# An encoder block on one core: later value products, a filled last stretch, a one-pass turn and a two-piece last store

## The chip, the cores and the metric

The kernel runs on one core of a Trainium2 chip. The metric is the device time of one launch in microseconds (us), the median of several runs. A core has TensorE (matrix products, with a weight load ahead of each), VectorE, ScalarE, GpSimd, SyncE (which here only issues transfers) and 16 DMA engines. The profile calls them PE, PEld, DVE, ACT, POOL and SP; SPq and ACTq are the transfers issued from SyncE and from ScalarE.

## The reference

One layer over 1024 rows of 1024 numbers, in float32:

```
h = x @ W_in                                   # q, k, v, z of two groups of 8 heads
y_a = neighborhood_attention(q_a, k_a, v_a)    # 16 x 64 grid, window 8 x 16, learned bias
y_b = windowed_gqa(rotary(q_b), rotary(k_b), v_b, sink)   # |i - j| <= 128
mixed = concat(y_a * silu(z_a), y_b * silu(z_b))
x = layer_norm(alpha * x + mixed @ W_out) * gain + bias
```

## The kernel before, in words

Every float32 factor is split into two float16 parts, high and low, and a product is made of three float16 products (high·high, high·low, low·high). The splits need scales, which come from maxima over the whole tensors.

**Opening.** The values of the first 512 rows are made while x is read in. Meanwhile VectorE reduces x to one maximum for each partition (`xm`, then `gm`). `x_turn` brings the 128 maxima of `gm` into every partition with one float32 product against the identity, `x_scale` takes the maximum of the result and works out the scale `xsc`, and `x1_hi` scales x with it for the float16 products that follow. The order of this part is the order in which it is written.

**Middle.** 128 attention units run in numbered steps: scores on TensorE, softmax on VectorE and ScalarE, then the probabilities, split in two, are turned by DMA transposes (L999, tile `tr`). Four units are a quad. The value product of quad q (`stage_pv`, L1035, 24 products) takes the turned probabilities and is put at the step that `PV_AT` gives; `stage_z` (L1046, VectorE) multiplies its result into the gate `z` at the step in `Z_AT`. Quads 30 and 31 are the last two. Between these steps `pump_to` feeds TensorE other products: first the projections (L404), then the head of the output projection (`out_head`, L1165), which can already use the four groups of gated results that are ready (`m4` to `m7`). `FILL_AT` and `FILL_N` say how many such products are fed by which step; what is left in the list comes after the last step, and `LO` is how many steps follow the last unit.

**End.** `final` splits the other four groups (`m0` to `m3`: cast on ScalarE L1076, difference on VectorE L1077, in halves of 512 rows) and the rest of the output weights (`wo8` to `wo15`: L1121/L1123, L1129/L1131), and finishes the output projection, 24 products for each of `m0` to `m3` over the eight sums that are open, then the row blocks 3 to 7 that have none yet. VectorE adds the residual, takes the statistics and normalises. Within `final` a scheduler with a model of the engines sets the order of the instructions, so it can differ from the order of the code.

**The last row block** (`norm_last`) has only its own time ahead of the end. Its first `NPE` columns go over TensorE: the normalised row is a product with a diagonal matrix `dg` (L1247) onto the bias, copied out by ScalarE (L1251) and stored from ScalarE's queue (L1252). The other columns go over VectorE in two operations (L1248, L1249) and are stored from SyncE's queue (L1250).

Of the kernel before, what the change touches and what calls it, by code (L numbers as in the profile page):

```python
# [13 lines left out]
ALU = mybir.AluOpType  # L14

S = 1024
D = 1024
# [21 lines left out]
SCALE_AT = ((4, 6), (7, 2))  # L39
K_ORDER = (5, 0, 6, 1, 7, 2, 3, 4)  # L40
FILL = ORDER[NPRO:]
FILL_AT = [0, 6.6, 13.4, 21.4, 29.4, 37.4, 45.4, 53.4, 61.4, 70, 78.8, 87.6, 96.4, 105, 113, 122, 125, 127, 128.5, 131.5, 136]
ZTAG = {"z3": "zv", "zb3": "zc", "z2": "zs", "zb1": "zd", "zb2": "ze"}
X2POOL = (1, 3, 5)
WVPOOL = (3, 5)
# [7 lines left out]
WO_MAX = 88  # L53
EO = (4, 5, 6, 7, 0, 1, 2, 3)
LAST = ((0, 384), (384, 128))
NPE = 384
PRE_AT = (12, 20)
WARP = (0, 0.33, 0.54, 0.86, 1)
QK_AT = 0.75
# [15 lines left out]
def hybrid_block(ctx, tc, xT, x, wt, wv, wo, bias, sink, gain, lbias, cos, sin, bmask, out):  # L75
    nc = tc.nc
# [10 lines left out]
    def bank(tag):  # L87
        bufs = {"pj": 2, "s": 5, "t": 1}[tag]
        return (ps1 if bufs == 1 else ps2).tile([128, 512], F32, tag=tag, name=f"ps_{tag}", bufs=bufs)
# [21 lines left out]
    def zslot(name, tag="z"):  # L111
        return zp.tile([128, S], F32, tag=tag, name=name, bufs=3 if tag == "z" else 1)
# [268 lines left out]
    def project(name):  # L381
        n = ORDER.index(name)
        w_split(2 * n + 2)
        for half in range(2):
            ps = new_group()
            for k in range(KT):
                if k % 4 == 0:
                    need(w_ops[2 * n + k // 4])
                h, l = parts[2 * n + k // 4]
                if n + 2 < NPRO and half == 0 and k == 4:  # L390
                    w_scan(2 * n + 4)
                if n + 2 < NPRO and half == 1 and k == 0:
                    w_scan(2 * n + 5)
                if half == 0 and k == 4:
                    w_split(2 * n + 3)
                if n + 2 < NPRO and half == 1 and k == 3:
                    z_tree(n + 2)
                if n + 2 < NPRO and half == 1 and k == 7:
                    w_scale(n + 2)
                for i, (a, b) in enumerate(((h, x16h), (h, x16l), (l, x16h))):  # L400
                    mv = b[half, k]
                    if name[0] == "q" and name[1] != "b":
                        mv = mv.rearrange("p (r b c) -> p b r c", b=4, r=8)
                    nc.tensor.matmul(ps, a[:, k % 4, :], mv,  # L404
                                     start=(k == 0 and i == 0), stop=(k == KT - 1 and i == 2))
                    if not (k == KT - 1 and i == 2):
                        yield
            groups.append(evac(name, half, ps))
            yield
# [26 lines left out]
    with ExitStack() as vctx:  # L436
# [76 lines left out]

        def x_turn(ps):
            nc.tensor.matmul(ps[:, 320:448], gm.to_broadcast([128, 128]), identf, start=False, stop=True,
                             skip_group_check=True)

        def x_scale(ps):
            nc.vector.tensor_reduce(gm, ps[:, 320:448], axis=AXX, op=ALU.max)
# [97 lines left out]
        for k in range(KT):  # L617
            if k + 3 < KT:
                ahead(k + 3)
            if k + 4 == KT:  # L620
                for j in range(KT):
                    nc.sync.dma_start(x1[j], xT[1, j])
                x_max(6, xh[6].bitcast(F32))
            for ps in FIRST if k == 0 else SECOND if k == 1 else ([(t, a, i) for i in range(3)] for t, a in T1):
                for t, a, i in ps:
                    lh, rh = ((xh, wvh), (xl, wvh), (xh, wvl))[i]
                    nc.tensor.matmul(banks[t, a][:, :320], lh[k][:, 128 * t:128 * t + 128],
                                     rh[k][:, 320 * a:320 * a + 320],
                                     start=(k == 0 and i == 0), stop=(k == KT - 1 and i == 2))
                if k > 1:  # L630
                    g = T1.index((t, a))
                    if (k, g) == SCALE_AT[0]:
                        wv_scale(banks[t, a])
                        for j in range(KT):
                            wv_hi(j)
                        x_max(7, xh[7].bitcast(F32))
                        for j in range(4):
                            x_max(8 + j, x1pair[j])
                        nc.vector.tensor_reduce(gm, xm, axis=AXX, op=ALU.max)
                        wv_lo(0)  # L640
                    if (k, g) == SCALE_AT[1]:
                        x_turn(banks[t, a])
                        x_scale(banks[t, a])
                        nc.vector.tensor_scalar(vo, vo, xrs, 0.5, op0=ALU.mult, op1=ALU.mult)
# [405 lines left out]
        at(WIN_AT[b], window, b)  # L1050
    run_to(48 * NPRO)
    fill.extend(project(n) for n in FILL)
    FILL_N = [48] * len(FILL) + [9, 9, 6, 12, 24]
    pumped = [0]

    def pump_to(u):
        n = 0
        k = int(u) % 4
        u = int(u) // 4 * 4 + 4 * (WARP[k] + (WARP[k + 1] - WARP[k]) * (u - int(u)))
        for k, c in enumerate(FILL_N):  # L1060
            u0, u1 = FILL_AT[k], FILL_AT[k + 1]
            n += int(c * min(max((u - u0) / (u1 - u0), 0), 1))
# [87 lines left out]
            m_ops[e].append(enq("pool", lambda h=h: nc.gpsimd.tensor_sub(  # L1150
                ml[e][:, h], zt[e][:, h], mh[e][:, h]), o))

    LO = 10
    NU = len(units)
    def out_mms(t, a, ps, es, c=None):
        o, w = (0, 512) if c is None else LAST[c]
# [25 lines left out]
    def final():  # L1182
# [15 lines left out]
        gb, bb = gain_tile[0], zslot("bb")  # L1198
# [19 lines left out]
        def row_stats(t):  # L1218
            mv = fp.tile([128, 2], F32, tag="mv", name="mv")
            nc.vector.bn_aggr(mv, stats[t][:, :4 if t == 7 else 2, :])  # L1220
            sd = fp.tile([128, 1], F32, tag="sd", name="sd")
            nc.scalar.activation(sd, mv[:, 1:2], AF.Sqrt, bias=eps, scale=ALPHA ** 2)  # L1222
            return mv, sd
# [9 lines left out]
        def norm_last(t):  # L1233
            ts = slice(128 * t, 128 * t + 128)
            xr = xrs[t]
            h0, h1 = slice(0, NPE), slice(NPE, D)
            ga = fp.tile([128, D], F32, name="ga", bufs=1)
            nc.scalar.mul(ga, gb, ALPHA)
            mv, sd = row_stats(t)
            ps = bank("t")  # L1240
            nc.tensor.matmul(ps[:, :NPE], identf, bb[:, h0], start=True, stop=False)
            nc.vector.scalar_tensor_tensor(xr[:, h0], xr[:, h0], mv[:, 0:1], ga[:, h0], op0=ALU.subtract, op1=ALU.mult)  # L1242
            rstd = fp.tile([128, 1], F32, tag="rstd", name="rstd")
            nc.vector.reciprocal(rstd, sd)
            dg = fp.tile([128, 128], F32, name="dg", bufs=1)
            nc.scalar.mul(dg, identf, rstd)
            nc.tensor.matmul(ps[:, :NPE], dg, xr[:, h0], start=False, stop=True)  # L1247
            nc.vector.scalar_tensor_tensor(xr[:, h1], xr[:, h1], mv[:, 0:1], ga[:, h1], op0=ALU.subtract, op1=ALU.mult)  # L1248
            nc.vector.scalar_tensor_tensor(xr[:, h1], xr[:, h1], rstd, bb[:, h1], op0=ALU.mult, op1=ALU.add)  # L1249
            nc.sync.dma_start(out[ts, h1], xr[:, h1])  # L1250
            nc.scalar.copy(xr[:, h0], ps[:, :NPE])  # L1251
            nc.scalar.dma_start(out[ts, h0], xr[:, h0])  # L1252

# [46 lines left out]
        with tc.manual_schedule():  # L1300
            norm_last(7)
# [17 lines left out]
        stage_mm(us)  # L1319

    PV_AT = {4 * q + 11: q for q in range(30)}
    PV_AT.update({131: 30, 135: 31})
    Z_AT = {4 * q + 13: q for q in range(30) if q not in (24, 25, 28, 29)}
    Z_AT.update({115: 24, 116: 25, 128: 28, 129: 29, 132: 30, 136: 31})

    clock["step"] = 0
    scan_ops = []
    for i in range(-LD, NU + LO):
        if 0 <= i + LD < NU:
# [162 lines left out]
```

## Time and profile before

| | us |
|---|---|
| median of 3 runs | 439.92 (439.67 to 441.48) |
| profiled execution, its own time | 441.73 |
| span of the profiled execution | 439.9 |
| TensorE busy in the span | 431.2 (98%) |
| VectorE | 347.8 (79%) |
| ScalarE | 298.8 (68%) |
| GpSimd | 212.7 (48%) |

The profile is of one execution, whose own time is 1.83 us longer than its span and 1.81 us longer than the median. Rows of the timeline give start, duration, engine, line, the operation with its result and operands, and how many were merged; a bracket gives the idle time ahead and what ended it. "x3" after a shape is a count of three.

### The profile page before, as it was taken

Reading aid. Unit: us, or ns where it says so; the run is one execution under the profiler, and the core shown is the slowest. Engines: PE = TensorE matmul, PEld = TensorE weight load, DVE = VectorE, ACT = ScalarE, POOL = GpSimd, SP = SyncE. Lnnn points to the kernel's source line nnn. Section 1 sums busy time; section 2 is a strip of 40 time slices with the busy share of each in tenths; the row PEclk is TensorE's granted clock in tenths of the full one; section 3 lists DMA queues with packets and bytes.
Section 4 is the critical chain, followed back from the end, with each engine's and each line's share of the span. In section 5 each row is a group of like instructions: output and inputs, shape, how many; then the busy total and the mean of one; then the engine's idle time right before and its main releaser. Section 6 shows DMA issues by size and latency. Waiting matters only on the chain. (4 is left out here: it accounts for less than half of the span.)

```text
span 439.9 us, 8798 instructions
## 1 busy us (share of the span) xinstructions
PE 431.2 (98%) x2955; PEld 233.2 (53%) x2955; DVE 347.8 (79%) x897; ACT 298.8 (68%) x697; POOL 212.7 (48%) x204
## 2 busy tenths in 40 slices
PE   9999999999999999999999999999999989999994
PEld 8987754444444545454545455554545544444442
DVE  5999947929989988988888887887879739089954
ACT  6798359877577988877889899879787756002211
POOL 0305743564845868356333455566652158005840
PEclk9999999999999999999999999999999999999999
DMA  8992088967946978776999899999999979101721
GB/s 296 343 339 71 5 259 250 302 247 254 322 113 136 168 147 171 141 145 143 173 154 201 138 190 223 192 202 217 216 208 225 193 166 363 41 1 72 262 74 72
DMA packets 133981, 81.72 MB, mean 186 GB/s; under 512 B 101296, under 2 KB 113328, under 8 KB 133680
## 3 DMA queue, kind: packets, MB, share of 16 engines
q1 hardware_dynamic: 133504, 80.67, 74.4%
q8 instruction: 23, 0.38, 0.3%
q10 hardware_dynamic: 432, 0.49, 0.3%
q14 instruction: 22, 0.18, 0.1%
HBM read 50.73 MB, written 9.96 MB: 138 GB/s over the span
## 5 line engine op out<-in xcount | busy, mean ns | idle before, releaser
L404 PE MATMUL ps_pj<-xf,wh 128*128 128x512 f16 x672 | 201.2, 379 | 0.0
L404 PE MATMUL ps_pj<-xf,wl 128*128 128x512 f16 x336 | 127.5, 380 | 0.0
L404 PEld LDWEIGHTS <-wh 128*128 128x128 f16 x672 | 64.9, 98 | 75.4 <-issue 0.8
L1165 PEld LDWEIGHTS <-m 128*128 128x128 f16 x408 | 38.7, 98 | 43.7
L974 ACT ACTIVATE ps_s<-sn,nm 128x385 f32<-128x385 f32 (+3 forms) x96 | 52.1, 543 | 13.9 <-DVE nm L958 12.5
L992 ACT ACTIVATE split<-ps_s,ri 128x384 f16<-128x384 f32 (+2 forms) x96 | 48.5, 539 | 18.3 <-ACT ps_s L974 11.7
L993 DVE SCALAR_TENSOR_TENSOR split<-ps_s,ri,split 128x384 f16<-128x384 f32 (+2 forms) x96 | 52.0, 570 | 5.6 <-ACT split L992 4.6
L1165 PE MATMUL ps_s<-wo,m 128*128 128x512 f16 (+1 forms) x240 | 53.3, 374 | 0.0
L404 PEld LDWEIGHTS <-wl 128*128 128x128 f16 x336 | 32.8, 98 | 38.5 <-issue 0.3
L219 POOL TENSOR_SCALAR wr<-wr,wsc 128x512 f32<-128x512 f32 x26 | 22.4, 862 | 46.9 <-ACT wh L214 45.5
L958 DVE CUSTOM_DVE_ANT_0 sn<-ps_s,bm,nsk 128x384 f32<-128x384 f32 (+1 forms) x64 | 39.7, 635 | 6.6 <-PE ps_s L933 6.4
L901 POOL TENSOR_SCALAR bias<-bias,rsg 128x552 f32<-128x552 f32 (+1 forms) x24 | 20.0, 834 | 45.8 <-DMA bias<-in_bias 33.9
L958 DVE CUSTOM_DVE_ANT_0 sn<-ps_s,bias,sg 128x264 f32<-128x264 f32 (+1 forms) x64 | 33.9, 543 | 2.3 <-PE ps_s L933 1.6
L933 PE MATMUL ps_s<-ks,qs 64*128 64x384 f16 (+4 forms) x384 | 33.4, 305 | 0.1
L220 POOL TENSOR_TENSOR wl<-wr,wh 128x512 f16<-128x512 f32 x26 | 31.8, 1223 | 2.2
L1222 ACT ACTIVATE sd<-mv,eps 128x1 f32<-128x1 f32 x8 | 2.4, 295 | 41.8 <-DVE mv L1220 39.5
L1264 POOL TENSOR_TENSOR xr<-xr,gb 128x512 f32<-128x512 f32 x7 | 11.2, 1607 | 35.9 <-ACT xr L1261 35.9
L993 DVE SCALAR_TENSOR_TENSOR split<-px,ri,split 128x384 f16<-128x384 f32 (+2 forms) x32 | 26.0, 812 | 2.5 <-ACT split L992 2.4
L933 PEld LDWEIGHTS <-qs 64*128 64x128 f16 x384 | 16.2, 94 | 19.5 <-issue 13.3
L681 PEld LDWEIGHTS <-xf 128*128 128x128 f16 x216 | 21.0, 98 | 8.5 <-DVE xf L535 0.3
L1165 PE MATMUL ps_pj<-wo,m 128*128 128x512 f16 (+1 forms) x120 | 24.2, 347 | 0.0
L681 PE MATMUL ps_s<-wf,xf 128*128 128x320 f16 x144 | 23.8, 299 | 0.0
(213 smaller groups left out, 791.0 us busy)
## 6 DMA issues: line engine op xcount, KB each, us to landing
ws<-in_wt SPq DMA_DIRECT2D x15, 512.0 KB, 5.2
wr<-in_wt SPq DMA_DIRECT2D x26, 256.0 KB, 2.9
bias<-in_bias SPq DMA_DIRECT2D x16, 276.0 KB, 3.3
wor<-in_wo SPq DMA_DIRECT2D x16, 256.0 KB, 3.6
xr<-in_x SPq DMA_DIRECT2D x8, 512.0 KB, 7.2
xraw<-in_xT SPq DMA_DIRECT2D x15, 256.0 KB, 5.0
out<-xr SPq DMA_DIRECT2D x14, 256.0 KB, 2.0
bias<-in_bias SPq DMA_DIRECT2D x8, 368.0 KB, 3.8
```

Source lines behind the costliest of these rows:

```text
L219: nc.gpsimd.tensor_scalar(raw, raw, scale, 1.0, op0=ALU.mult, op1=ALU.mult)
L220: nc.gpsimd.tensor_sub(l, raw, h)
L404: nc.tensor.matmul(ps, a[:, k % 4, :], mv, start=(k == 0 and i == 0), stop=(k == KT - 1 and i == 2))
L681: nc.tensor.matmul(ps[:, :320], lh[t // 4, k][:, 128 * (t % 4):128 * (t % 4) + 128], rh[k][:, 320 * a:320 * a + 320], start=(k == first an ...
L901: op = enq("pool", lambda: nc.gpsimd.tensor_scalar(bv, bv, rsg, -1.0, op0=ALU.mult, op1=ALU.mult), ld, prio=0)
L933: nc.tensor.matmul(st[u, "ps"][:, :m], *parts[i], start=i == 0, stop=i == 2)
L958: nc.vector.tensor_tensor_reduce(sn[:, :m], ps[:, :m], bias_t, sg[:, c:c + 1], init, op0=ALU.add, op1=ALU.min, accum_out=nm)
L974: nc.scalar.activation(pt[:, :m], sn[:, :m], AF.Exp, bias=nm, scale=-1.0, accum_out=sm)
L992: nc.scalar.activation(hl[:, :m, 0, :c], src, AF.Copy, scale=ri)
L993: nc.vector.scalar_tensor_tensor(hl[:, :m, 1, :c], src, ri, hl[:, :m, 0, :c], op0=ALU.mult, op1=ALU.subtract)
L1165: nc.tensor.matmul(ps, lh[:, ts], rh[:, cs], start=(e == EO[0] and i == 0), stop=(e == EO[-1] and i == 2))
L1264: nc.gpsimd.tensor_mul(xr[:, h1], xr[:, h1], gb[:, h1])
```

## The change

Three places change. In the opening, `x_turn` is marked as a transpose. In the middle, the value products of quads 30 and 31 move from steps 131 and 135 to 133 and 138, their `stage_z` from 132 and 136 to 135 and 139, three more steps follow the last unit, and 24 products more of `out_head` are fed within steps 136 to 140.5, where they were left for after the last step. In the last row block TensorE's share falls from 384 to 320 columns, VectorE's grows from 640 to 704, and the second of VectorE's two operations and its store come in two pieces of 352 columns.

```diff
-FILL_AT = [0, ..., 125, 127, 128.5, 131.5, 136]
+FILL_AT = [0, ..., 125, 127, 128.5, 131.5, 136, 140.5]
-NPE = 384
+NPE = 320
         def x_turn(ps):
             nc.tensor.matmul(ps[:, 320:448], gm.to_broadcast([128, 128]), identf, start=False, stop=True,
-                             skip_group_check=True)
+                             is_transpose=True, skip_group_check=True)
-    FILL_N = [48] * len(FILL) + [9, 9, 6, 12, 24]
+    FILL_N = [48] * len(FILL) + [9, 9, 6, 12, 24, 24]
-    LO = 10
+    LO = 13
-            nc.vector.scalar_tensor_tensor(xr[:, h1], xr[:, h1], rstd, bb[:, h1], op0=ALU.mult, op1=ALU.add)
-            nc.sync.dma_start(out[ts, h1], xr[:, h1])
+            for c in (slice(NPE, 672), slice(672, D)):
+                nc.vector.scalar_tensor_tensor(xr[:, c], xr[:, c], rstd, bb[:, c], op0=ALU.mult, op1=ALU.add)
+                nc.sync.dma_start(out[ts, c], xr[:, c])
-    PV_AT.update({131: 30, 135: 31})
+    PV_AT.update({133: 30, 138: 31})
-    Z_AT.update({115: 24, 116: 25, 128: 28, 129: 29, 132: 30, 136: 31})
+    Z_AT.update({115: 24, 116: 25, 128: 28, 129: 29, 135: 30, 139: 31})
```

On VectorE, ScalarE, GpSimd and SyncE the order of instructions stays as it was, but for the pieces in the last row block. On TensorE three stretches are reordered. The first is ahead of quad 30's value product, whose weights are `va3_2` and whose turned probabilities are `tr`; the rows with `m4` to `m7` are products of `out_head` into the sums of row blocks 2 (`ps_s_5134`), 3 (`ps_s_5164` before, `ps_s_5167` now) and 4 (`ps_s_5168` now).

```order
 L1165 MATMUL ps_s_5134<-wo2_4493,m7_4027 128x512
 L1165 LDWEIGHTS m4_3343
-L1165 MATMUL ps_s_5164<-wo0_4316,m4_3343 128x512
+L1165 MATMUL ps_s_5167<-wo0_4316,m4_3343 128x512
...
+L1165 MATMUL ps_s_5168<-wo0_4316,m4_3343 128x512
...
+L1165 MATMUL ps_s_5167<-wo0_4316,m5_3562 128x512
...
+L1165 MATMUL ps_s_5168<-wo0_4316,m5_3562 128x512
...
+L1165 MATMUL ps_s_5167<-wo2_4493,m6_3795 128x512
 L1035 LDWEIGHTS va3_2_4851
 L1035 MATMUL ps_t_1842<-tr_4977,va3_2_4851 64x256
```

Twelve products more now stand between quad 29's value product and quad 30's: 28 where there were 16.

The second stretch is around quad 31's value product (weights `va3_3`) on TensorE, before:

```order
L1165 MATMUL ps_s_5165<-wo2_4493,m7_4027 128x512
L1035 LDWEIGHTS va3_3_4958
L1035 MATMUL ps_t_1842<-tr_5072,va3_3_4958 64x256
...
L1165 MATMUL ps_s_5245<-wo4_5131,m4_3343 128x512
...
L1165 MATMUL ps_t_5343<-wo4_5131,m4_3343 128x512
```

and now, where `ps_s_5220` and `ps_s_5233` are the second halves of row blocks 0 and 1, whose weights are `wo4` to `wo7`:

```order
L1165 MATMUL ps_s_5220<-wo4_5131,m4_3343 128x512
...
L1165 MATMUL ps_s_5220<-wo6_5153,m7_4027 128x512
...
L1165 MATMUL ps_s_5233<-wo4_5131,m5_3562 128x512
L1035 LDWEIGHTS va3_3_4958
L1035 MATMUL ps_t_1842<-tr_5072,va3_3_4958 64x256
...
L1165 MATMUL ps_t_5343<-wo4_5131,m4_3343 128x512
```

Between quads 30 and 31 there are now 27 products of `out_head` where there were 22, and 20 between quad 31 and the first product with `m0` where there were 37; the sum of the three, 75, is the same.

The third stretch is the block of `m0` on TensorE, whose products with row block 4 (`ps_s_5165` before, `ps_s_5168` now) read the second half of `m0`. Before, they closed the block of `m0`; now they stand inside that of `m1`, the last of them 37 products after the block's start:

```order
L1165 MATMUL ps_s_5167<-wo8_5291,m0_5279 128x512
...
L1165 MATMUL ps_pj_4995<-wo10_5299,m1_5280 128x512
...
L1165 MATMUL ps_s_5168<-wo8_5291,m0_5279 128x512
...
L1165 MATMUL ps_s_5134<-wo10_5299,m1_5280 128x512
L1165 LDWEIGHTS m0_5279
L1165 MATMUL ps_s_5168<-wo8_5291,m0_5279 128x512
```

The high·high products of the other sums now stand ahead of the rest of their products in that block.

More of the change, by code (lines that the diff above doesn't have):

```diff
@@ L41 @@
 FILL = ORDER[NPRO:]
-FILL_AT = [0, 6.6, 13.4, 21.4, 29.4, 37.4, 45.4, 53.4, 61.4, 70, 78.8, 87.6, 96.4, 105, 113, 122, 125, 127, 128.5, 131.5, 136]
+FILL_AT = [0, 6.6, 13.4, 21.4, 29.4, 37.4, 45.4, 53.4, 61.4, 70, 78.8, 87.6, 96.4, 105, 113, 122, 125, 127, 128.5, 131.5, 136, 140.5]
 ZTAG = {"z3": "zv", "zb3": "zc", "z2": "zs", "zb1": "zd", "zb2": "ze"}
```

## Prediction

> **What bounds the kernel now.** I read the page first, then the list of waits, the chain of work that ended last, and the timeline of TensorE around every gap.
>
> ```profile
> PE 431.2 (98%) x2955; PEld 233.2 (53%) x2955; DVE 347.8 (79%) x897; ACT 298.8 (68%) x697; POOL 212.7 (48%) x204
> ```
>
> TensorE is busy for 431.2 of 439.9 us. The number of its products hardly changes, so time can come only from the 8.7 us in which it is idle. The waits say where two pieces of that lie:
>
> ```profile
> PE ps_t L1247 <- ACT dg L1246: 1.5, 1, 1.5
> PE ps_t L1035 <- DMA tr<-split: 1.5, 1, 1.5
> ```
>
> The first is in the last row block, the second at a value product that waits for turned probabilities. The chain that ended last runs through that second wait:
>
> ```profile
> 351.04 3.65 DMA tr<-split
> 354.68 0.14 issue
> ```
>
> TensorE's own timeline shows it as a hole. L1035 rows are the value products of quads 29, 30 and 31, in this order; all others are products of the output projection:
>
> ```profile
> 349.70 0.82 PE L1165 MATMUL ps_pj<-wo,m 128*128 128x512 f16 x3
> 350.36 2.97 PE L1165 MATMUL ps_s<-wo,m 128*128 128x512 f16 x13
> 354.82 1.18 PE L1035 MATMUL ps_t<-tr,va 128*64 128x256 f16 x24 [1.49 <-DMA tr<-split]
> 355.93 4.92 PE L1165 MATMUL ps_s<-wo,m 128*128 128x512 f16 x22
> 360.78 1.18 PE L1035 MATMUL ps_t<-tr,va 96*64 96x256 f16 x24
> 361.89 5.57 PE L1165 MATMUL ps_s<-wo,m 128*128 128x512 f16 x25
> 367.30 2.75 PE L1165 MATMUL ps_t<-wo,m 128*128 128x512 f16 x12
> 369.89 0.81 PE L1165 MATMUL ps_pj<-wo,m 128*128 128x512 f16 x3
> ```
>
> From here on starts are compared, since ends are modelled. One product takes 0.216 us: 25 of them from 361.89 to 367.30. The 16 products from 349.70 are through at 349.70 + 16 x 0.216 = 353.16, and quad 30 begins at 354.82, so the hole is 1.66 us. The change of shape takes a little in any case: 22 products from 355.93 end at 360.68 and quad 31 begins at 360.78, 0.10 later. What filling the hole can bring is therefore 1.66 - 0.10 = 1.56 us. A value product takes 1.11 us (354.82 to 355.93).
>
> **Middle: quads 30 and 31 later.** No operation is added or removed. Twelve products move ahead of quad 30: 12 x 0.216 = 2.59 us. TensorE comes to quad 30 at 353.16 + 2.59 + 0.10 = 355.85, while the chain has its probabilities landed at 354.68. The margin is 1.17 us. How steady landings are:
>
> ```profile
> L999 SPq DMA_TRANSPOSE tr<-split x12: 1210/1229/2112, 339.6 to 357.1; - x12
> DMA to landing us min/median/max: 2.7/3.3/4.6
> ```
>
> Even the slowest of these twelve, 4.6 us after an issue at 351.04, would be there at 355.64, ahead of TensorE. SyncE's order is unchanged, and `tr` has three quads' buffers, so no transpose waits for the two products that move. Quad 30 then ends at 356.96, 27 products bring quad 31 to 356.96 + 5.83 + 0.10 = 362.89 (2.1 us later than before), it ends at 364.00, and after 20 more the block of `m0` begins at 368.32, against 369.89: 1.57 us earlier. I take 1.57 as the gain, if nothing that is wanted earlier or made later is now the late one. What could be:
>
> ```profile
> 357.97 1.16 POOL L1134 TENSOR_TENSOR wo<-wor,wo 128x512 f16<-128x512 f32 x1
> 365.77 6.29 POOL L1129 TENSOR_TENSOR wo<-wor,wo 128x512 f16<-128x512 f32 x4
> 362.01 0.48 DVE L1046 SCALAR_TENSOR_TENSOR z<-ps_t,zcol,z 128x256 f32<-128x256 f32 x1 [5.49 <-PE ps_t L1035]
> 369.39 1.65 DVE L1131 SCALAR_TENSOR_TENSOR wo<-wor,wos,wo 128x512 f16<-128x512 f32 x1
> 370.96 3.45 DVE L1077 TENSOR_TENSOR m<-z,m 128x512 f16<-128x512 f32 x4
> 362.00 2.92 SPq L1205 DMA_DIRECT2D xr<-in_x  x6
> 386.28 0.75 DVE L1215 SCALAR_TENSOR_TENSOR xr<-ps_pj,oinv,xr 128x512 f32<-128x512 f32 x1 [11.87 <-PE ps_pj L1165]
> ```
>
> - Wanted earlier: the products with `wo4` to `wo7` now precede quad 31. GpSimd ends the last of these weights at 357.97 + 1.16 = 359.13; TensorE reads it 20 products after quad 30, at 356.96 + 4.32 = 361.3. Margin 2.2 us. `wo9` is the first of GpSimd's four from 365.77, done at about 367.3, and is read with its low part 13 products into the block of `m0`, at 371.1.
> - Made later: VectorE's `stage_z` of quad 31 follows quad 31, so it moves from 362.01 to 364.05, and behind it in VectorE's order stand nine operations up to the first of the four L1077 from 370.96, the second half of `m0`. That is done before by 370.96 + 1.64 = 372.60 at the latest (1.65, the dearest row beside it), so 2.04 later by 374.64. TensorE wants it 37 products into the block, at 368.32 + 7.99 = 376.3. Margin 1.7 us; this is the tightest place. ScalarE does not move, since its casts here follow GpSimd and loads.
> - The six loads of x start when quad 31 ends (362.00), so at 364.0; they are first used at 386.28 - 1.57.
>
> From 386 on VectorE follows TensorE with the same distance (its 11.87 us wait ends with TensorE), so the 1.57 us reach the last row block.
>
> **Opening: the turn as a transpose.**
>
> ```profile
> 28.02 0.88 DVE L512 SCALAR_TENSOR_TENSOR wf<-wvraw,wvs,wf 128x640 f16<-128x640 f32 x1
> 28.15 0.49 PE L515 MATMUL ps_s<-identf,gm 128*128 128x128 f32 x2
> 28.40 0.54 PE L627 MATMUL ps_s<-wvh,x 128*128 128x320 f32 x2
> 28.81 0.28 DVE L519 TENSOR_REDUCE gm<-ps_s 128x1 f32<-128x128 f32 x1
> 30.43 12.61 PEld L681 LDWEIGHTS <-xf 128*128 128x128 f16 x94 [0.30 <-DVE xf L535]
> 63.45 0.27 PE L719 MATMUL ps_s<-identf,vg 128*128 128x128 f32 x1
> 63.56 0.38 PE L404 MATMUL ps_pj<-xf,wh 128*128 128x512 f16 x1
> ```
>
> The turn is two passes now and holds TensorE for 28.40 - 28.15 = 0.25 us. L719 is such a transpose, of `vg`: one pass, 63.56 - 63.45 = 0.11 us. So TensorE saves 0.14 us, but then waits 0.14 us longer at 30.43 for `xf`. That tile comes from the scale, the scale from L519, and L519 starts at 28.81 as L512 ahead of it on VectorE ends (28.90, the next one being taken some 0.09 early), not when the turn ends (28.15 + 0.49 = 28.64). Sum: 0, bounds -0.14 and 0.
>
> **The last row block.**
>
> ```profile
> 433.33 0.62 DVE L1242 SCALAR_TENSOR_TENSOR xr<-xr,mv,ga 128x384 f32<-128x384 f32 x1
> 433.94 0.87 DVE L1248 SCALAR_TENSOR_TENSOR xr<-xr,mv,ga 128x640 f32<-128x640 f32 x1
> 434.05 0.40 ACT L1246 ACTIVATE dg<-identf,rstd 128x128 f32<-128x128 f32 x1 [0.37 <-DVE rstd L1244]
> 434.51 0.91 PE L1247 MATMUL ps_t<-xr,dg 128*128 128x384 f32 x2 [1.53 <-ACT dg L1246]
> 434.84 0.89 DVE L1249 SCALAR_TENSOR_TENSOR xr<-xr,rstd,bb 128x640 f32<-128x640 f32 x1
> 435.50 0.48 ACT L1251 COPY xr<-ps_t 128x384 f32<-128x384 f32 x1 [1.05 <-PE ps_t L1247]
> 435.75 0.33 SPq L1250 DMA_DIRECT2D out<-xr  x1
> 436.01 0.36 ACTq L1252 DMA_DIRECT2D out<-xr  x1
> out<-xr SPq DMA_DIRECT2D x3, 256.0 KB, 2.0
> out<-xr SPq DMA_DIRECT2D x1, 320.0 KB, 2.2
> out<-xr ACTq DMA_DIRECT2D x1, 192.0 KB, 2.5
> ```
>
> (The last three rows give size and us from issue to landing.) A VectorE column costs (0.87 - 0.62) / 256 = 0.98 ns. L1242 loses 64 columns (-0.06), L1248 gains 64 (+0.06), so the second operation still starts at 434.84. Its first piece of 352 takes about 0.59, and its store issues at 435.45 instead of 435.75; the second ends at about 435.95, its store issues at 435.97. TensorE's path: `dg` 0.06 earlier, the product 0.91 x 320/384 = 0.76 (-0.15), the copy 0.40 (-0.08), together -0.29 at most and -0.06 if neither shrinks; I take -0.27, issue at 435.74 instead of 436.01. Before, the last landing is 436.01 + 2.5 = 438.51. Now ScalarE's store lands at 435.74 + 2.5 = 438.24; SyncE's second, between 2.0 and 2.5 after its issue, lands from 437.97 to 438.47. I take 438.24, since 2.0 to 2.2 are SyncE's rows, and so 0.27 of gain; bounds 0.04 and 0.51.
>
> A rule of the Trainium skill speaks against the split: "DMA: Bandwidth & Descriptors", section "Anatomy of one DMA — SWDGE (gpsimd) path", gives each transfer a fixed 2.0 us beside bytes / 436e3, and "Rules for kernel authors" advises to coalesce. By that fit (for another issuing path) the second piece would land at 438.38 where the whole one landed at 438.50, and the gain would be an estimated 0.1 us. The row of 320 KB, landed in 2.2 us, does not agree with the fit's 2.75.
>
> **Sum.** 1.57 + 0 + 0.27 = 1.84 us. The profiled execution's own 441.73 would become 439.89. It lies 1.81 above the median; from the median, 439.92 - 1.84 = **438.08**. With the bounds of the unknown costs (hole 1.4 to 1.66, turn 0 to 0.14, store 0.04 to 0.51) the forecast spans 437.6 to 438.5.
>
> **The rivals.**
> - *The hole is smaller in an ordinary run.* The profiled execution is 1.81 us above the median, about the size of the hole. If the quickest landing (2.7) were the ordinary one, the hole would end at 353.74 rather than 354.68, 0.94 us less: gain 1.84 - 0.94 = 0.9, 439.0 us; with no hole at all 439.65. For it: 441.48 among the three plain runs, so some runs do differ by this much. Against it: the instruction that issued at 351.04 depends on on-chip work that is the same in every run.
> - *More comes out than the sum.* The turn's 0.14 counts after all, if the scale follows the turn, and the store gives its upper 0.51: 439.92 - 1.57 - 0.14 - 0.51 = 437.7. Against it: L519 starts right behind L512. The Trainium skill, "Perfetto Trace Analysis", section "Transposes", asks for a logical transpose to be issued as one; L719 beside L515 agrees with it on TensorE, but not on the path.
> - *VectorE becomes the late one: slower.* Its nine operations from 364.05 up to the second half of `m0` take 14.85 us if every one costs 1.65, the row beside a busy GpSimd. Then that half is there at 379.4, TensorE waits 3.1 us at 376.3, and the time is 439.92 - 1.84 + 3.1 = 441.2. It decides against the change from 376.3 + 1.84 = 378.1 on. Against it: GpSimd is busy only until 365.77 + 6.29 = 372.06.
> - *The change does nothing.* The products stand before quad 30, but their operands or sums are late and the wait only moves: 439.92 less the store's 0.27, 439.65. The sums' banks were last read by the softmax of units done before the hole; little speaks for it.
>
> **How the numbers follow.** About 0.5% (2.2 us) is what a measurement here can tell from no change, so faster means below 437.72 and slower above 442.12. The forecast has 0.66, the smaller hole 0.14, more than the sum 0.10, VectorE late 0.06, nothing 0.04. Of the forecast I put 0.12 below 437.72; with the second rival that is 0.22 faster. Half of VectorE late, where the wait is over 4 us instead of 3.1, is slower: 0.03. The rest, 0.75, is within. The range reaches from 437.4 (the second rival, with a spread of a few tenths as between 439.67 and 439.92) to 439.8, which takes in the smaller hole and no effect, and leaves out VectorE late and the outer ends.
>
> **What would show it.** Right: no wait of L1035 for `tr`; quad 30 near 355.9, quad 31 near 362.9, the first product with `m0` near 368.3, each counted from an unchanged 349.7; no wait of TensorE from there to the last row block; L519 still right behind L512 and the wait at `xf` 0.4 instead of 0.3; three stores issued 0.3 us earlier to 0.04 us earlier than the last of before. Wrong: a new bracket on a PE row of L1165, above all on an `m0` weight; a hole left at quad 30; a last landing no earlier, measured from the last product.

## The result, and the profile after

| | before | after |
|---|---|---|
| median, us | 441.39 (20 runs, 439.67 to 442.58) | 440.12 (20 runs, 438.90 to 441.87) |
| profiled execution, own time | 441.73 | 439.95 |
| its span | 439.9 | 438.2 |

The ratio of the times is 0.997, with a 95% interval of 0.9956 to 0.9985: 1.3 us less, between 0.66 and 1.94 (each times 441.39). So the change makes the kernel faster, by less than the 0.5% that the prediction had set as its bound. The 20 runs of before hold the three that the prediction started from (439.67, 439.92, 441.48); the other seventeen lie between 440.88 and 442.58.

The profile's first part and the waits of TensorE, after. The 1.5 us wait for `tr` is gone; a 0.2 us one is left:

```profile
PE 430.6 (98%) x2954; PEld 233.0 (53%) x2954; DVE 347.3 (79%) x898; ACT 299.0 (68%) x697; POOL 210.3 (48%) x204
PE ps_t L1247 <- ACT dg L1246: 1.6, 1, 1.6
PE ps_t L681 <- DVE xf L535: 0.2, 1, 0.2
PE ps_t L1035 <- DMA tr<-split: 0.2, 1, 0.2
```

TensorE's timeline after, in the middle (start, duration, line, shapes, count). The L1035 rows are quads 29, 30 and 31:

```profile
348.60 1.18 PE L1035 MATMUL ps_t<-tr,va 128*64 128x256 f16 x24 [0.17 <-DMA tr<-split]
349.71 0.82 PE L1165 MATMUL ps_pj<-wo,m 128*128 128x512 f16 x3
350.37 5.56 PE L1165 MATMUL ps_s<-wo,m 128*128 128x512 f16 x25
355.86 1.18 PE L1035 MATMUL ps_t<-tr,va 128*64 128x256 f16 x24
356.97 6.00 PE L1165 MATMUL ps_s<-wo,m 128*128 128x512 f16 x27
362.90 1.18 PE L1035 MATMUL ps_t<-tr,va 96*64 96x256 f16 x24
365.75 2.75 PE L1165 MATMUL ps_t<-wo,m 128*128 128x512 f16 x12
368.34 0.59 PE L1165 MATMUL ps_pj<-wo,m 128*128 128x512 f16 x2
```

Quad 30 begins at 355.86 without a wait, quad 31 at 362.90, the block of `m0` at 368.34: forecast were 355.85, 362.89 and 368.32. VectorE and GpSimd behind it, after (the last row is the second half of `m0` to `m3`):

```profile
364.13 0.48 DVE L1046 SCALAR_TENSOR_TENSOR z<-ps_t,zcol,z 128x256 f32<-128x256 f32 x1 [6.56 <-PE ps_t L1035]
364.53 5.85 POOL L1129 TENSOR_TENSOR wo<-wor,wo 128x512 f16<-128x512 f32 x4
373.38 2.49 DVE L1077 TENSOR_TENSOR m<-z,m 128x512 f16<-128x512 f32 x4
```

The first of the four operations from 373.38 on makes the second half of `m0`. At a quarter of 2.49 us each it is done at 374.0; the forecast was 374.64 at the latest, and TensorE wanted it at 376.3. No row of L1165 has a bracket: nothing became late there.

The opening after, where L519 again starts right behind L512 on VectorE (28.39 + 0.88 = 29.27), not when the turn ends (28.53 + 0.32 = 28.85):

```profile
28.31 0.17 DVE L639 TENSOR_REDUCE gm<-xm 128x1 f32<-128x12 f32 x1
28.39 0.88 DVE L512 SCALAR_TENSOR_TENSOR wf<-wvraw,wvs,wf 128x640 f16<-128x640 f32 x1
28.53 0.32 PE L515 MATMUL ps_s<-identf,gm 128*128 128x128 f32 x1
29.18 0.28 DVE L519 TENSOR_REDUCE gm<-ps_s 128x1 f32<-128x128 f32 x1
30.80 0.25 PEld L681 LDWEIGHTS <-xf 128*128 128x128 f16 x3 [0.45 <-DVE xf L535]
```

The wait at `xf` went from 0.30 to 0.45 us, as the 0.14 us saved on TensorE predicts.

The last row block: first the start of the last 24 products before, then that start, the last operations and the landings after:

```profile
430.77 1.50 PE L1165 MATMUL ps_pj<-wo,m 128*128 128x128 f16 x24
```

```profile
429.22 1.50 PE L1165 MATMUL ps_pj<-wo,m 128*128 128x128 f16 x24
433.29 1.08 DVE L1250 SCALAR_TENSOR_TENSOR xr<-xr,rstd,bb 128x352 f32<-128x352 f32 x2
433.90 0.83 SPq L1251 DMA_DIRECT2D out<-xr  x2
434.24 0.35 ACTq L1253 DMA_DIRECT2D out<-xr  x1
DMA to landing us min/median/max: 1.9/2.1/2.3
out<-xr ACTq DMA_DIRECT2D x1, 160.0 KB, 2.1
```

SyncE's first piece lands in 1.9 us, so its second, issued at 433.90 + 0.83 - 0.33 = 434.40, in 2.3: at 436.70, 7.48 us behind the start of the last 24 products. Before it was 438.51 - 430.77 = 7.74.

### The profile page after: what moved, and what is told of

Read it like the earlier page. It is cut to its first block, busy times and chain, and to the rows that moved or that the text cites. A ratio compares the mean times of both kernels' runs of the same rounds, so it can differ in the third digit from the quotient of the medians.

```text
span 438.2 us, 8799 instructions
## 1 busy us (share of the span) xinstructions
PE 430.6 (98%) x2954; PEld 233.0 (53%) x2954; DVE 347.3 (79%) x898; ACT 299.0 (68%) x697; POOL 210.3 (48%) x204
## 5 line engine op out<-in xcount | busy, mean ns | idle before, releaser
L404 PE MATMUL ps_pj<-xf,wh 128*128 128x512 f16 x672 | 201.2, 379 | 0.0
L404 PE MATMUL ps_pj<-xf,wl 128*128 128x512 f16 x336 | 127.5, 380 | 0.0
L404 PEld LDWEIGHTS <-wh 128*128 128x128 f16 x672 | 64.8, 98 | 75.4 <-issue 0.8
L1165 PEld LDWEIGHTS <-m 128*128 128x128 f16 x408 | 38.7, 98 | 43.7
L1165 PE MATMUL ps_s<-wo,m 128*128 128x512 f16 (+1 forms) x240 | 53.3, 374 | 0.0
L404 PEld LDWEIGHTS <-wl 128*128 128x128 f16 x336 | 32.8, 98 | 38.5 <-issue 0.3
L993 DVE SCALAR_TENSOR_TENSOR split<-px,ri,split 128x384 f16<-128x384 f32 (+2 forms) x32 | 24.7, 771 | 2.1 <-ACT split L992 1.9
L1165 PE MATMUL ps_pj<-wo,m 128*128 128x512 f16 (+1 forms) x120 | 24.2, 347 | 0.0
```

What stands on the lines that cost most here:

```text
L404: nc.tensor.matmul(ps, a[:, k % 4, :], mv, start=(k == 0 and i == 0), stop=(k == KT - 1 and i == 2))
L993: nc.vector.scalar_tensor_tensor(hl[:, :m, 1, :c], src, ri, hl[:, :m, 0, :c], op0=ALU.mult, op1=ALU.subtract)
L1165: nc.tensor.matmul(ps, lh[:, ts], rh[:, cs], start=(e == EO[0] and i == 0), stop=(e == EO[-1] and i == 2))
```

## Where the time of a run lies

Five marks cut ten of the fourteen profiled runs into stretches (left out are the two kernels with repeated products and the two in which quad 29 waits for VectorE): the first product L404, the value product of quad 22 (the first L1035 row behind 300 us), the start of the block of `m0`, the start of the last 24 products, and the end of the span. Each column is the difference to the mark before it, in us.

| kernel | to L404 | to quad 22 | to `m0` | to the last 24 | to the end |
|---|---|---|---|---|---|
| before | 60.00 | 242.85 | 67.04 | 60.88 | 9.15 |
| before, turn alone | 59.53 | 242.40 | 66.65 | 60.88 | 9.15 |
| before, residue moved | 60.54 | 242.50 | 67.67 | 60.88 | 9.15 |
| before, last row block alone | 59.23 | 242.40 | 71.30 | 60.88 | 8.97 |
| before, middle alone | 59.34 | 242.39 | 66.26 | 60.88 | 9.14 |
| after | 60.37 | 242.39 | 65.58 | 60.88 | 8.95 |
| after, one piece | 59.45 | 242.40 | 65.63 | 60.88 | 9.26 |
| after, residue moved | 59.40 | 243.24 | 65.84 | 60.88 | 8.94 |
| after, quad 29 later, mended | 59.85 | 242.40 | 65.95 | 60.88 | 8.96 |
| the same, residue moved | 60.31 | 242.91 | 65.48 | 60.88 | 8.96 |

From `m0` to the last 24 products every run takes the same 60.88 us. What varies from run to run of the same code is ahead of it: 1.3 us in the opening, 0.85 up to quad 22, and the stretch that the change is about. There the four runs with the old order take 66.65 to 71.30 (the middle two 67.04 and 67.67), the four with the new order and quad 29 where the change has it 65.58 to 66.26. The end is 0.19 us shorter with two pieces: 9.15 on the mean of four old ends, 8.96 on that of five new ones with two pieces.

## The experiments

**The middle alone, and the last row block alone.** The kernel before with one part of the change each:

```diff
-    PV_AT.update({131: 30, 135: 31})
+    PV_AT.update({133: 30, 138: 31})
```

(with the other lines of the middle), and

```diff
-NPE = 384
+NPE = 320
```

(with the two pieces).

> Only the middle part of the change: quads 30 and 31 at steps 133 and 138, 24 products more fed in the steps, three more steps. Theory 1 (the sum of the prediction holds in ordinary runs): 1.56 us less than before, no wait for the turned probabilities at quad 30, quad 30 near 355.9 and the first product with m0 near 368.3 on the profile's scale. Theory 2 (the hole of the profiled execution is larger than that of an ordinary run): 0.5 to 1.1 us less. Theory 3 (the middle gives its 1.56 and another part of the change takes 0.5 us back): 1.56 us less or slightly more, and one of the other parts alone is slower than before.

> Only the last row block's part: TensorE's share 320 columns, VectorE's second operation and store in two pieces. Theories 1 and 2: 0.27 us less (0.04 to 0.51), the hole at quad 30 still there; a difference of this size is mostly below what the times can tell, so the profile decides: the last landing, counted from the start of the last 24 products, 0.2 to 0.5 us earlier than before's 438.51 - 430.77 = 7.74. Theory 3, if this part is the one that costs: 0.3 to 0.6 us more.

Measured: the middle alone 440.03 us, ratio 0.9975 (0.9959 to 0.9992), so 1.1 us less than before's 441.07, between 0.35 and 1.8. The last row block alone 440.82, ratio 0.9986 (0.9963 to 1.0009): unclear by itself, but its end is 8.97 us in the profile where the middle alone has 9.14. The profiled run of the second, at 444.56 the longest of its 13, happens to show what the old order does when transposes come late. TensorE's quads 29 and 30 there:

```profile
348.81 1.18 PE L1035 MATMUL ps_t<-tr,va 128*64 128x256 f16 x24 [0.56 <-DMA tr<-split]
356.24 1.96 PE L1035 MATMUL ps_t<-tr,va 128*64 128x256 f16 x24 [2.68 <-DMA tr<-split]
```

The code of this stretch and the data are the same, and the wait is 2.7 us instead of 1.5. It is not a constant of the kernel.

**How large the hole is in ordinary runs.** The first product of row block 2, repeated ahead of quad 30 in the kernel before. Each repeat starts the same sum anew:

```diff
+                if (t, a, e, i) == (2, 0, EO[0], 0):
+                    for _ in range(5):
+                        nc.tensor.matmul(ps, lh[:, ts], rh[:, cs], start=True, stop=True)
```

and the same with 10. They are free as long as they fit into the hole.

> Before, with the first product of row block 2 (which opens its sum, 3 products after quad 29) written five times more, each overwritten by the next: 5 x 0.216 = 1.08 us more work for TensorE ahead of quad 30. Theory 1: the hole of 1.56 us takes it up, the time stays within 0.2 us and the wait at quad 30 shrinks to about 0.4. Theory 2, with an ordinary hole of 0.5 to 1.1 us: up to 0.6 us more. If there were no hole in ordinary runs: 1.08 us more.

> As the kernel with five, with ten products more: 2.16 us of work ahead of quad 30. Theory 1: 2.16 - 1.56 = 0.6 us more than before. Theory 2: 1.1 to 1.7 us more. No hole: 2.16 us more. The time over before, taken from 2.16, is the size of the hole in ordinary, unprofiled runs.

Measured: 5 repeats (1.08 us) 441.11, ratio 0.9996 (0.9977 to 1.0014): nothing that the times can tell. In its profile quad 30 does not wait at all, where a wait of 0.4 us was expected, so in that run the hole was at most 1.08 us. 10 repeats (2.16 us) 442.16, ratio 1.0017 (1.0 to 1.0033): 0.75 us, between 0 and 1.5. So the hole holds 2.16 - 0.75 = 1.4 us, between 0.7 and 2.2; the forecast's 1.56 fits, and so does a smaller hole. In the profile of the 10 repeats quad 29 waits, and quad 30, which now has 26 products ahead of it, does not:

```profile
348.91 1.18 PE L1035 MATMUL ps_t<-tr,va 128*64 128x256 f16 x24 [1.60 <-DMA tr<-split]
355.74 1.18 PE L1035 MATMUL ps_t<-tr,va 128*64 128x256 f16 x24
```

That does not show that quad 29's wait used up the hole. Without the repeats TensorE would have come to quad 30 at 355.74 - 2.16 = 353.58, and VectorE read the result of quad 29, which lies in the same tile, until 354.87: some 1.3 us of hole would have been left.

**Quad 29 later.** What is left to wait for at quad 29, 0.2 us in the changed kernel and 0.6 in the run above, should go if that product also stood two steps later. On the changed kernel:

```diff
-    PV_AT.update({133: 30, 138: 31})
+    PV_AT.pop(127)
+    PV_AT.update({129: 29, 133: 30, 138: 31})
-    Z_AT.update({115: 24, 116: 25, 128: 28, 129: 29, 135: 30, 139: 31})
+    Z_AT.update({115: 24, 116: 25, 128: 28, 131: 29, 135: 30, 139: 31})
...
-        if i in PV_AT or i % 4 == 3 and i + 1 < NU:
+        if i in PV_AT or i % 4 == 3 and i < NU:
```

The last line keeps the softmax sums of step 127, which has no value product any more, where they were.

> The changed kernel, with quad 29's value product at step 129 instead of 127 and its stage_z at 131, so that 24 products of the head instead of 16 stand ahead of quad 29 and 20 instead of 28 between quads 29 and 30: TensorE comes to quad 29 1.73 us later. Theory 2b (the landing of the transposes varies from run to run, and what the change does not take up of it is now waited for at quad 29: 0.17 us in the trace of after, 0 to 1.6 us in the others): no wait at quad 29, on average some 0.4 us less than the changed kernel, 1.4 to 1.9 us less than before, and a smaller distance between the lowest and the highest run. Theory 1 (the spread comes from ahead of this stretch, the loads of the opening): as the changed kernel within 0.1 us, and the same spread.

Measured: 445.19, ratio 1.0064 (1.0039 to 1.0089): slower, a miss. Quad 29 on TensorE, and what it waited for on VectorE:

```profile
353.17 2.13 PE L1035 MATMUL ps_t<-tr,va 128*64 128x256 f16 x24 [3.68 <-DVE z L1046]
352.64 0.48 DVE L1046 SCALAR_TENSOR_TENSOR z<-ps_t,zcol,z 128x256 f32<-128x256 f32 x1
```

Step 128 now puts `stage_z` of quad 28 ahead of quad 29's product. Both quads use halves of one tile `ps_t`, and the wait is by the tile: TensorE stood 3.68 us until VectorE had read the other half, at 352.64 + 0.48 = 353.12, behind the softmax of four units. "PSUM — Partial Sum Buffer" of the Trainium skill, section "PSUM bank collisions raise a hardware error", asks for such a wait, by the bank and not by the address; this is what it costs when the reader is far back in its queue. The mended form reads quad 28 behind quad 29's product:

```diff
-    Z_AT.update({115: 24, 116: 25, 128: 28, 131: 29, 135: 30, 139: 31})
+    Z_AT.update({115: 24, 116: 25, 130: 28, 131: 29, 135: 30, 139: 31})
```

> The changed kernel with the value product of quad 29 two places later (step 129 instead of 127) and VectorE's stage_z of quads 28 and 29 at steps 130 and 131, so that stage_z of quad 28 no longer stands ahead of quad 29's product. Theory (what still varies is the landing of the transposes that quads 29 and 30 wait for; the wait of 3.7 us for z in the run with quad 29 later came from two quads sharing one bank of ps_t): no wait for z, no wait of quad 29 for tr, and 0.2 to 0.4 us below the changed kernel, ratio near 0.996 of the kernel before. Rival (stage_z of quads 28 and 29 are late on VectorE wherever they stand, because the softmax is queued ahead of them): the wait for z moves to quad 30 or to the first product that reads m0, 1 us or more, and the time is above the changed kernel's.

Measured: 439.47 (439.26 to 440.56), ratio 0.9957 (0.9942 to 0.9973). No wait for z. Quads 29 and 30 on TensorE:

```profile
349.70 1.18 PE L1035 MATMUL ps_t<-tr,va 128*64 128x256 f16 x24
355.72 1.18 PE L1035 MATMUL ps_t<-tr,va 128*64 128x256 f16 x24 [0.41 <-DMA tr<-split]
```

The wait at quad 29 is gone, and one of 0.41 us stands at quad 30, which has 20 products ahead of it instead of 28. In this run quad 30's transposes also landed later (53.3 us behind quad 22's start, 51.4 in the changed kernel), so one look does not say how much of that wait is the edit's. This version beats the kernel before. Against the changed kernel it stands 0.6 us lower (0.9957 and 0.997 of 441.4), but the intervals overlap, and the two were not run side by side: open.

**The opening: what holds the scale back.** On the changed kernel, the low part of the first weights (L512, `wv_lo(0)`) goes behind the scaling of x, so that nothing stands between L639 and L519 on VectorE:

```diff
                         nc.vector.tensor_reduce(gm, xm, axis=AXX, op=ALU.max)
-                        wv_lo(0)
...
-        for k in range(1, KT):
+        for k in range(KT):
             wv_lo(k)
```

> The changed kernel, with the first of VectorE's residues of the value weights (L512, 0.88 us), which stands ahead of the maximum that takes up the turn, moved behind the scaling of x. The prediction's reason for a turn worth nothing (L512 holds the maximum back, not the turn): the maximum starts 0.05 us after the turn's end instead of 0.33 us, TensorE's wait at xf (0.45 us) shrinks to 0.1 to 0.2, about 0.25 us off the time, which is at the limit of what the times show. Rival (the turn and the maximum are not on the path): the wait at xf stays at 0.3 to 0.45.

Measured: 440.23, ratio 0.9955 (0.9933 to 0.9977), whose interval overlaps that of the changed kernel, so that the profile decides. L519 now waits for the turn itself:

```profile
28.27 0.29 DVE L519 TENSOR_REDUCE gm<-ps_s 128x1 f32<-128x128 f32 x1 [0.41 <-PE ps_s L515]
29.90 0.39 PEld L680 LDWEIGHTS <-xf 128*128 128x128 f16 x4 [0.17 <-DVE xf L535]
```

From L639 (27.69 there) to the scaled x are 29.90 - 27.69 = 2.21 us, against 30.80 - 28.31 = 2.49 in the changed kernel: L512 was what held the scale back, as the prediction read it. The same edit on the kernel before, with the turn in two passes, and the turn alone without the edit:

> The kernel before with the residue moved behind the scaling of x, the turn left in two passes. Theory: L519 now waits for the turn, so the time from L639 to the first product of the scaled x falls, by 0.28 us less the 0.14 us of the second pass, to about 2.35 us. Rival (the move does all of it and the turn nothing): 2.2 us. One more look at the unchanged middle too, as in the run with the turn alone.

> The kernel before with the turn of x's maxima as a transpose and nothing else. Theory (L512 holds L519 back): the time from L639 to the first product of the scaled x stays at 2.5 us, L519 starts right behind L512 and TensorE waits 0.4 to 0.5 us there. Rival: it falls by 0.14 us. The profile is also one more look at the unchanged middle: by the theory of landings that vary, the hole at quad 30 is between 0.5 and 2.7 us, not the same 1.49 again.

Measured (one run each, 442.52 and 440.42). With the edit and two passes, L515 at TensorE and L519 at VectorE:

```profile
28.02 0.49 PE L515 MATMUL ps_s<-identf,gm 128*128 128x128 f32 x2
28.54 0.29 DVE L519 TENSOR_REDUCE gm<-ps_s 128x1 f32<-128x128 f32 x1 [0.58 <-PE ps_s L515]
```

L639 to the scaled x is 30.18 - 27.80 = 2.38 us: the one-pass turn is worth 2.38 - 2.21 = 0.17 us there, the theory's 0.14. The turn alone missed its expectation of 2.5 us:

```profile
27.24 0.17 DVE L639 TENSOR_REDUCE gm<-xm 128x1 f32<-128x12 f32 x1
28.03 0.27 PE L515 MATMUL ps_s<-identf,gm 128*128 128x128 f32 x1
28.34 0.29 DVE L519 TENSOR_REDUCE gm<-ps_s 128x1 f32<-128x128 f32 x1
```

Here `gm` was ready at 27.41, and TensorE came to the turn only at 28.03, behind products that its order puts first. So L519 starts as the turn ends (28.30), and the scaled x is there 29.98 - 27.24 = 2.74 us behind L639. Which of the two is late, L512 or TensorE, changes from run to run: in the first of the two runs that follow, TensorE comes to the turn 0.9 us behind `gm`, and the scaled x is there 30.40 - 27.38 = 3.02 us behind L639 in spite of the edit.

Both edits together, first with the quad 29 that waits for z, then mended:

> Both: quad 29 later and the residue moved. If both theories hold, 0.4 + 0.25 us below the changed kernel, 2 us below before (0.9955); if neither, as the changed kernel.

> The same, with the residue of the first weight part moved behind the scaling of x as in the run with the residue first. Theory: both gains add: 0.28 us from the opening, 0.2 to 0.4 us from quad 29, so ratio near 0.995 of the kernel before and 0.5 to 0.7 us below the changed kernel. Rival (opening gain is taken up by a later wait in the opening): no more than 0.4 us below.

Measured: 445.81, ratio 1.008 (1.0051 to 1.0109), the same 3.7 us wait; and 440.05, ratio 0.9966 (0.9949 to 0.9984), which is no better than either edit alone. The opening's gain is given back some 20 us later. VectorE has as much to do as before and now stands idle for 0.41 us while the turn runs, so it comes to its two L559 18.90 us behind L639 (46.64 - 27.74), against 18.40 in the changed kernel. TensorE's product L261 of a later weight scale waits for VectorE's L264, which stands behind the two L559. First TensorE, VectorE and GpSimd in the mended one, then VectorE and GpSimd in the changed kernel with the edit alone:

```profile
46.61 0.69 POOL L556 TENSOR_SCALAR xraw<-xraw,xsc 128x512 f32<-128x512 f32 x1
46.64 2.77 DVE L559 SCALAR_TENSOR_TENSOR xf<-xraw,xsc,xf 128x512 f16<-128x512 f32 x2
49.33 0.28 DVE L264 TENSOR_REDUCE zc<-ps_t 128x1 f32<-128x128 f32 x1
49.66 0.22 PE L261 MATMUL ps_t<-cs,ones 128*128 128x128 bf16 x1 [0.70 <-DVE zc L264]
```

```profile
46.57 1.24 POOL L556 TENSOR_SCALAR xraw<-xraw,xsc 128x512 f32<-128x512 f32 x1
46.60 1.75 DVE L559 SCALAR_TENSOR_TENSOR xf<-xraw,xsc,xf 128x512 f16<-128x512 f32 x2
```

With the edit, L261 does not wait where the two L559 take 1.75 us, and waits 0.7 where they take 2.77. Without it there is no such wait in the changed kernel, though they take 2.77 there. From L639 to the first L404 it is 59.40 - 27.69 = 31.71 us with the edit and quick L559, against 31.96 without the edit in the two profiles of new orders whose L559 are as quick; with slow L559 it is 60.31 - 27.74 = 32.57, against 60.37 - 28.31 = 32.06 in the changed kernel. So the edit gains 0.25 us or loses 0.5: the rival had it right that a later wait in the opening takes the gain. Which it is goes with GpSimd's L556, which starts 0.02 to 0.03 us ahead of the first L559 in every profile: in four of the fourteen L556 takes 1.24 us and the two L559 1.75, in the other ten 0.69 and 2.77. One of the two engines is quick at the other's cost; what decides which one is not shown.

**The last store in one piece.** On the changed kernel:

```diff
-            for c in (slice(NPE, 672), slice(672, D)):
+            for c in (slice(NPE, D),):
```

> The changed kernel with VectorE's 704 columns in one operation and one store. Counted from the start of the last 24 products: in the changed kernel SyncE's last issue ends at 5.51 us and the span at 8.98, before at 5.60 (ScalarE's) and 9.13. By the prediction's step the split is what lets VectorE's share grow: one piece would be ready 0.12 us earlier than the two (0.95 against 1.08) but its 352 KB land in 2.2 to 2.3 us; the span would end at 8.9 to 9.1. By the rule that each transfer pays its own fixed cost, the one piece is the faster: 8.8 or below.

Measured: one run, 439.41; its end is 9.26 us, against 8.96 with two pieces, so neither forecast held. The stores and their landings:

```profile
433.38 0.38 ACTq L1253 DMA_DIRECT2D out<-xr  x1
433.41 0.33 SPq L1251 DMA_DIRECT2D out<-xr  x1
out<-xr SPq DMA_DIRECT2D x1, 352.0 KB, 2.7
out<-xr ACTq DMA_DIRECT2D x1, 160.0 KB, 2.9
```

The two stores are issued within 0.03 us and take 2.7 and 2.9; in the changed kernel, with three stores 0.16 to 0.34 us apart, it was 1.9, 2.1 and 2.3. "DMA: Bandwidth & Descriptors" of the Trainium skill, section "Rules for kernel authors", has transfers from several engines share the same DMA engines, and these rows agree, though VectorE's store is also twice as large here. The split is worth 0.30 us on one look; the share of 320 columns without it would be worth nothing (9.26 against 9.15).

## Why the prediction was right and wrong

- **The middle: right in these two profiles.** Quads 30 and 31 and the block of `m0` came within 0.02 us of their forecast, no wait took the hole's place, and the margins held. Between the two profiles the stretch from quad 22 to `m0` fell by 67.04 - 65.58 = 1.46 us: 1.56 less of hole and 0.15 less ahead of quad 28, 0.25 given back ahead of quad 29.
- **The opening: right, 0.** The turn's 0.14 us went into the wait at `xf` in these profiles. It counts only where L512 does not hold L519 back. That a run may differ in this was not seen.
- **The last row block: right in the total, by luck in the working.** The last landing was forecast at 7.47 us behind the start of the last 24 products (438.24 - 430.77) and came at 7.48, though by SyncE's second piece and not by ScalarE's store, which took 2.1 us and not 2.5. The end came 0.19 us earlier (mean of the table) against the 0.27 forecast. The upper bound of 0.51 does not follow from the working, by which ScalarE's store alone lands 0.27 us earlier than before.
- **The sum against the profiled run: right, in part by luck.** 441.73 - 1.84 = 439.89 forecast, 439.95 measured. Of these 1.78 us the middle and the end make 1.46 + 0.20; the rest is what the stretches that the change hardly touches differed by in these two runs, 0.37 us longer to the first L404 and 0.46 shorter from there to quad 22.
- **The step that failed: "from the median, 439.92 - 1.84".** The median of three runs was not the time of the kernel before, which is 441.39 over 20 runs, 1.47 us more: two of the three lie below all seventeen that followed, and the medians of before in three later sets were 441.07, 441.62 and 441.63. From 441.39 the same sum gives 439.55, and the range moved with it, 438.9 to 441.3, holds 440.12. The prediction saw the sign, a profiled run 1.81 us above the median "about the size of the hole", and took the run for the odd one; the median was. Why two of the three were low stays open: of the 83 runs in the three later sets 5 are below 440, so two in three would be a rare draw.
- **The term that was too large: the middle's 1.57 us, with 1.4 and 1.66 as the bounds of the hole** (the 1.4 stands there without a working). In the old order quad 30 starts when the last of three things is there: TensorE (1.11 + 16 x 0.216 + 0.10 us behind quad 29's start), quad 30's last transpose (0.13 behind its landing), and VectorE's reading of quads 28 and 29 from `ps_t` (0.05 behind its end). In the four profiles of the old order without repeats (waits of 0.83, 1.13, 1.49 and 2.68 us) this gives the measured starts within 0.01 us. In the changed kernel's profile TensorE would have come at 353.27; the last transpose landed at 354.19, and VectorE read until 354.58:

```profile
353.72 0.86 DVE L1046 SCALAR_TENSOR_TENSOR z<-ps_t,zcol,z 128x256 f32<-128x256 f32 x2
```

  So the old order would have started quad 30 at 354.63 there, 1.36 us late: that is what the move was worth in that run, provided that neither VectorE's reading nor the landing goes by the order of the products that moved. By the same working it was worth 0.9 to 1.6 us in nine of the ten profiles that have quad 29 in its old place (in two of them with the repeats taken off), and 2.6 in the tenth (the last row block alone). The median is 1.27, 0.3 less than the prediction took from one run. With the end's 0.19 the sum is 1.46; 1.27 was measured, between 0.66 and 1.94, and what is left is inside that interval.
- **The rivals.** "The hole is smaller in an ordinary run" was right in the main. The argument against it, on-chip work that is the same in every run, does not hold: quad 30's last transpose was issued 47.2 to 50.9 us behind quad 22's start in these ten profiles. "No hole at all" did not occur, and in six of the ten it is VectorE's reading that comes last, at which the prediction did not look. One of them is the kernel before with the residue moved, where the transposes had landed at 355.27:

```profile
354.71 0.87 DVE L1045 SCALAR_TENSOR_TENSOR z<-ps_t,zcol,z 128x256 f32<-128x256 f32 x2
355.63 1.18 PE L1034 MATMUL ps_t<-tr,va 128*64 128x256 f16 x24 [0.83 <-DVE z L1045]
```

  VectorE reads until 355.58. "VectorE becomes the late one" did not come, but quad 29 later shows that VectorE's queue is a real danger one edit on, through a tile and not through `m0`. "The change does nothing" and "more comes out than the sum" are refuted by the profile.

## What to carry to other kernels

A sum worked out from one profiled run belongs on that run's own time; three plain runs that differ by 0.4% do not give a base to a quarter of that. A hole that waits for transfers varies from run to run, so its size is read from several profiles, and for every operand that may be the last: filling it brings no more than the latest of them allows. When a product is moved, see who else writes or reads its output tile: the reader of the other half may stand ahead of it now.

## What the runs showed of the hardware

- The landing of a DMA transpose here is not a constant: from 342 us on, medians of 2.8, 3.2, 3.5 and 3.5 us in four profiles (turn alone, before, after, last row block alone), with extremes of 2.7 and 4.8. SyncE's last eight took 11.62 us to issue in the first and 12.40 in the last.
- Two L559 on VectorE, the same instructions on the same data, take 1.75 us in four of the fourteen profiles and 2.77 in ten. GpSimd's L556, which starts 0.02 to 0.03 us ahead of them, takes 1.24 us in those four and 0.69 in those ten.
